# Low parts of weight units: a negated copy and an accumulating DMA in place of a subtraction

## The chip, the cores and the metric

The kernel runs on one core of a Trainium2 chip. What is compared is device time in microseconds of the whole program, one inference step of a two-layer network; the times shown are medians of several runs, and the profile is one execution of its own.

## The reference

One step of a hybrid network over 512 latent and 128 context tokens, 1024 channels wide. Layer 0 mixes tokens by windowed attention beside a convolution module, layer 1 by a gated recurrence in both directions; each layer then has a squared-ReLU MLP of 4096 hidden channels. Every sub-layer is modulated by shift, scale and gate vectors made from a condition vector by large `w_mod` matrices. Cut to what matters:

```
for li in range(2):
    mp, ms = adaln(c_ctx, w_mod[li], b_mod[li]), adaln(c, w_mod[li], b_mod[li])
    h = modulate(y, norm_mix[li], shift, scale)            # RMSNorm, then (1 + scale), + shift
    o = attention_and_conv(h, att_in, att_out, ...)        # li = 0
    o = rg_lru(h, lru_in, lru_out, lru_wa, lru_wx, ...)    # li = 1: conv4, gates, scans both ways
    y = y + gate * o
    y = y + gate2 * (square(relu(modulate(y, ...) @ w_ff1[li])) @ w_ff2[li])
return rmsnorm(y_prompt), rmsnorm(y_sample), new_k, new_v, new_h
```

All of it is in fp32.

## The kernel before

Channels lie on the 128 partitions, the 640 tokens along the free dimension. TensorE multiplies in fp32r, a shortened fp32. To keep fp32 accuracy each operand is cut into a high part (the value rounded to fp32r) and a low part (the value less its high part), and a product is three matmuls: high x high, high x low and low x high. The low part of the weight is named `wlo`, the high part `whi`; those of the activations are `hh` and `hl` (normed input), `fh` and `fl` (hidden), `xh` and `xl` (recurrent gates), `yh` and `yl`.

Weights come in units of 128 x 1024 numbers, 512 KB. `weights` (L101) makes one ready: SyncE loads it into `wraw` (three buffers, and a fourth in the MLPs), ScalarE rounds it into `whi`, and VectorE subtracts: `wlo = wraw - whi`. Both parts have three buffers each (`parts_tile`, L94). A whole unit feeds 48 matmuls (`product`, L115). 118 units are made whole. In the second projection of the MLP (`down`, L814) units are used by halves of 128 x 512, as seven sums and differences of a fast block product; `ready` (L789) cuts each half into the same three buffers, two halves to one. A half feeds 12 matmuls.

The order of work is set by a scheduler that goes by priority and its own cost figures; each engine then runs its list strictly in order. `weights` asks for a priority raised by an `offset`: 4000 in general, 0 for the first six units of attention (L346, L353 and `att_unit`, L381). With 4000 the loading and cutting of a unit stand as early in the lists as their buffers allow.

Places the text speaks of:
- The MLP goes through four groups `g` of eight hidden units `f`. Unit `f = 0` of the next group is multiplied before `down(g)`, and unit `f = 1` inside it, in `between` (L888), just before the last half block, `fourth` (L862). `bu` are two PSUM banks that hold partial sums in `down`.
- The recurrent layer starts with `rec(0)` (L957). Its units are multiplied in the order written in `ORDER`; `gates` (L986) needs ScalarE to free PSUM by `tanh` (tiles `ra`, `ib`), `rec` and `gate_br` need VectorE (tile `bs` is its last step). GpSimd clears the edges of `rp` and copies the last column of each scan into `nst_t` (L1037); it issues no DMA.
- The last four units are those of `ws` (L897), multiplied by halves of the tokens at the very end.

Of the kernel before, what the change touches and what calls it, by code (L numbers as in the profile page):

```python
# [12 lines left out]
AF = mybir.ActivationFunctionType  # L13
ALU = mybir.AluOpType
# [22 lines left out]
def backbone(ctx, tc, vecs, xT, wmod, w_att, w_ao, w_ff1, w_ff2, w_li, w_lo, w_lg, kcT, vc,  # L37
             ident_d, mask_d, rope_d, yo, nkT, nvT, nst):
    nc = tc.nc
# [25 lines left out]
    def sub_lo(out, full, hi):  # L65
        nc.vector.tensor_tensor(out, full, f32(hi), op=ALU.subtract)  # L66
# [18 lines left out]
    def raw_unit(ap):  # L85

        if more and next(unit_) % 4 == 3:
            raw = more[0].tile([128, 1024], F32, name="wraw", tag="wraw")
        else:
            raw = wp.tile([128, 1024], F32, name="wraw", tag="wraw", bufs=3)  # L90
        nc.sync.dma_start(raw, ap)
        return raw

    def parts_tile():  # L94
        return tuple(wp.tile([128, 1024], F32R, name=n, tag=n, bufs=3) for n in ("whi", "wlo"))

    def split(hi, lo, raw):
        nc.scalar.activation(hi, raw, AF.Copy)  # L98
        sub_lo(lo, raw, hi)

    def weights(ap, offset=4000, own=None):  # L101
        with tc.high_priority(offset=offset):
            raw = raw_unit(ap)
            hi, lo = parts_tile() if own is None else (own[:, 0], own[:, 1])
            split(hi, lo, raw)
        return hi, lo


# [235 lines left out]

    first_mods(1, range(W0))
    early = [weights(w_att[0], 0)]  # L346
    first_mods(1, range(W0, 8))
    for k in range(0, 8, 2):
        nc.sync.dma_start(x[:, k:k + 2], xT[:, k:k + 2])
    nm = Norm(ap_, SC[0, 0])  # L350
    for k in range(8):
        nm.scaled(k)
    early += [weights(w_att[1], 0), weights(w_att[2], 0)]  # L353
    for k in range(8):
        nm.square(k)
# [25 lines left out]
    def att_unit(i):  # L381
        wh, wl = weights(w_att[i], 0 if i < WL else 4000)
        p = P2()
        product(p, wh, wl, range(8), rhs)
        return p
# [811 lines left out]
```

## Time and profile before

| | us |
|---|---|
| median of 3 runs | 1446.51 (1446.1 to 1448.87) |
| profiled execution, its own time | 1449.23 |
| span of that execution | 1447.5 |
| TensorE busy | 1409.2 |
| VectorE busy | 1042.9 |
| ScalarE busy | 734.5 |
| GpSimd busy | 89.8 |

The span goes from the first to the last instruction of the program. The profile is read in this order: how busy each engine is, who waited for whom, then the timeline at the places where one unit's parts are made and used. PE is TensorE, DVE VectorE, ACT ScalarE, POOL GpSimd.

### The profile page before, as it was taken

The numbers are of one execution on the slowest core, as the hardware profiler recorded it, in microseconds if no ns is written. First come the engines' busy times: TensorE is split into PE (matmuls) and PEld (weight loads), VectorE is DVE, ScalarE is ACT, GpSimd is POOL, SyncE is SP. The second block draws the span as 40 slices with busy tenths as digits, with TensorE's granted clock in tenths as the row PEclk, the third lists the DMA queues.
The fourth block names the chain that finished last, engine by engine and source line by source line (L and its number), as shares of the span: only waits on it lengthen the run. The fifth ranks groups of instructions, "written<-read, shape, count | busy, mean of one in ns | idle before, by whom it ended". The sixth has DMA issues, their size and how long they took to land.

```text
span 1447.5 us, 23697 instructions
## 1 busy us (share of the span) xinstructions
PE 1409.2 (97%) x9567; PEld 1316.9 (91%) x9567; DVE 1042.9 (72%) x1885; ACT 734.5 (51%) x1174; POOL 89.8 (6%) x126
## 2 busy tenths in 40 slices
PE   6999999999999999999999999999999999999998
PEld 4898674999999999999989999899999999999997
DVE  6699794675765675675588699997676676676673
ACT  5343467455534533533555878835643543543553
POOL 1000760000000000000000023200000000000000
PEclk9998999999999999999999999999999999999999
DMA  8523506224253244334213122122213213113112
GB/s 320 204 74 126 175 1 204 88 95 140 86 183 138 93 142 168 109 131 163 72 59 103 59 73 72 61 74 88 74 46 119 70 59 116 60 59 117 45 59 73
DMA packets 42908, 151.87 MB, mean 105 GB/s; under 512 B 4912, under 2 KB 5680, under 8 KB 42800
## 3 DMA queue, kind: packets, MB, share of 16 engines
q1 hardware_dynamic: 42800, 150.38, 30.1%
q8 instruction: 75, 1.23, 0.3%
q14 instruction: 33, 0.27, 0.1%
HBM read 147.60 MB, written 2.76 MB: 104 GB/s over the span
## 4 chain that ended last, share of the span: by engine, by line
PE 85%; DVE 7%; DMA 3%; ACT 3%; issue 1%; POOL 1%; SPq 0%; ACTq 0%; POOLq 0%; DVEq 0%
PE p L113 65%; PE bu L113 11%; PE p L292 3%; DMA mraw<-in_wmod 3%; PE p L435 2%; DVE wlo L66 1%; PE p L617 1%; DVE xc L976 1%; DVE ib L1035 1%; PE p L613 1%; ACT whi L98 1%; PE p L581 1%; PE p L583 0%; DVE t L1027 0%; DVE ib L1028 0%
## 5 line engine op out<-in xcount | busy, mean ns | idle before, releaser
L98 ACT ACTIVATE whi<-wraw 128x512 fp32r<-128x512 f32 (+1 forms) x327 | 246.5, 779 | 451.8 <-PE p L113 331.5
L113 PE MATMUL p<-hh,whi 128*128 128x320 f32 (+1 forms) x1512 | 462.1, 313 | 2.9 <-ACT hh L186 1.7
L113 PE MATMUL p<-hl,whi 128*128 128x320 f32 (+1 forms) x1512 | 459.8, 311 | 0.2 <-DVE hl L187 0.2
L113 PE MATMUL p<-hh,wlo 128*128 128x320 f32 (+1 forms) x1512 | 349.8, 310 | 0.0
L66 DVE TENSOR_TENSOR wlo<-wraw,whi 128x512 fp32r<-128x512 f32 (+1 forms) x327 | 279.5, 877 | 43.7 <-ACT whi L98 42.2
L113 PEld LDWEIGHTS p<-hh,whi 128*128 128x128 f32 x1512 | 285.6, 189 | 15.4 <-issue 7.8
L113 PEld LDWEIGHTS p<-hl,whi 128*128 128x128 f32 x1512 | 286.0, 189 | 0.9 <-DVE hl L187 0.8
L113 PEld LDWEIGHTS p<-hh,wlo 128*128 128x128 f32 x1512 | 256.4, 189 | 0.9 <-issue 0.8
L113 PE MATMUL p<-fh,whi 128*128 128x320 f32 x528 | 167.0, 316 | 3.9 <-ACT fh L98 1.1
L113 PE MATMUL p<-fl,whi 128*128 128x320 f32 x528 | 163.8, 310 | 2.0 <-DVE fl L66 2.0
L113 PE MATMUL p<-fh,wlo 128*128 128x320 f32 x528 | 163.6, 311 | 0.7 <-DVE wlo L66 0.7
L142 DVE SCALAR_TENSOR_TENSOR x<-p,mod,x 128x320 f32<-128x320 f32 (+2 forms) x228 | 96.1, 448 | 58.6 <-PE p L113 55.8
L268 DVE TENSOR_TENSOR fr<-p,R 128x640 f32<-128x640 f32 x64 | 52.6, 822 | 101.7 <-PE p L113 101.7
L113 PE MATMUL bu<-fh,whi 128*128 128x320 f32 x360 | 113.2, 314 | 0.3 <-ACT bu L841 0.3
L113 PEld LDWEIGHTS p<-fh,whi 128*128 128x128 f32 x528 | 99.9, 189 | 14.0 <-issue 5.1
L113 PE MATMUL bu<-fl,whi 128*128 128x320 f32 x360 | 112.3, 312 | 0.0
L113 PE MATMUL bu<-fh,wlo 128*128 128x320 f32 x360 | 112.1, 311 | 0.0
L740 ACT ACTIVATE fr<-fr,bs 128x512 f32<-128x512 f32 (+1 forms) x128 | 65.2, 555 | 78.5 <-DVE bs L270 78.3
L113 PEld LDWEIGHTS p<-fl,whi 128*128 128x128 f32 x528 | 100.0, 189 | 2.4 <-DVE fl L66 2.4
L113 PEld LDWEIGHTS p<-fh,wlo 128*128 128x128 f32 x528 | 99.6, 189 | 1.5 <-DVE wlo L66 1.5
L416 DVE SCALAR_TENSOR_TENSOR z<-u,vt,z 128x655 f32<-128x655 f32 x90 | 79.3, 904 | 0.4
L292 PE MATMUL p<-mraw,base 128*32 128x256 f32 x768 | 66.0, 418 | 12.8 <-DMA mraw<-in_wmod 7.8
(227 smaller groups left out, 2084.7 us busy)
## 6 DMA issues: line engine op xcount, KB each, us to landing
wraw<-in_w_ff SPq DMA_DIRECT2D x128, 512.0 KB, 3.5
mraw<-in_wmod SPq DMA_DIRECT2D x96, 512.0 KB, 4.1
wraw<-in_w_li SPq DMA_DIRECT2D x16, 512.0 KB, 3.4
wraw<-in_w_att SPq DMA_DIRECT2D x14, 512.0 KB, 3.6
wraw<-in_w_ao SPq DMA_DIRECT2D x8, 512.0 KB, 3.5
wraw<-in_w_lo SPq DMA_DIRECT2D x8, 512.0 KB, 3.4
x<-in_xT SPq DMA_DIRECT2D x4, 640.0 KB, 9.1
wraw<-in_w_lg SPq DMA_DIRECT2D x4, 512.0 KB, 3.5
```

The costliest lines, as they stand in the source:

```text
L66: nc.vector.tensor_tensor(out, full, f32(hi), op=ALU.subtract)
L98: nc.scalar.activation(hi, raw, AF.Copy)
L113: nc.tensor.matmul(o, w, v, start=start, stop=stop, **kw)
L142: nc.vector.scalar_tensor_tensor(v, src[:, a:b], gate[:, n, s:s + 1], v, op0=ALU.mult, op1=ALU.add)
L268: nc.vector.tensor_tensor(hy(o), p[:, :, 0:320], R, op=ALU.mult)
L292: nc.tensor.matmul(p[32 * q:32 * q + 32, half * 256:half * 256 + 256], base[:, kt], raw[:, q * 256:q * 256 + 256], start=(kt == 0), stop=( ...
L416: nc.vector.scalar_tensor_tensor(z, u[:, k:k + 655], wv[:, k:k + 1], z, op0=ALU.mult, op1=ALU.add)
L435: nc.tensor.matmul(p[:, 0:328], dg[:, d], u[:, o + k:o + k + 328], start=(k + i == 0), stop=(k == 30 and i == 2))
L581: nc.tensor.matmul(o, qh[:, g, qs], KH, start=True, stop=False)
L613: nc.tensor.transpose(pt[:, b.kv, g * 128:g * 128 + 128], b.S[g][:, j * 128:j * 128 + 128], ident)
L617: nc.tensor.matmul(pav[c], vv[:, sl, c], th[:, b.kv], start=(j == 0), stop=(j == len(vs) - 1))
L740: nc.scalar.activation(r[:, a:b], r[:, a:b], AF.Relu, bias=bs[:, q:q + 1])
```

## The change

For units asked for with the offset of 4000, `weights` no longer subtracts on VectorE. ScalarE writes the rounded weight into `whi`, then the same rounded weight with the opposite sign into `wlo`; a DMA issued by GpSimd then reads the raw unit from memory a second time and adds it onto `wlo`, which leaves raw less rounded. The six units of the start and all half units keep the subtraction.

```
         with tc.high_priority(offset=offset):
             raw = raw_unit(ap)
             hi, lo = parts_tile() if own is None else (own[:, 0], own[:, 1])
-            split(hi, lo, raw)
+            if offset == 4000:
+                nc.scalar.activation(hi, raw, AF.Copy)
+                nc.scalar.activation(lo, raw, AF.Copy, scale=-1.0)
+                nc.gpsimd.dma_start(lo, ap, accum_op=ALU.add)
+            else:
+                split(hi, lo, raw)
         return hi, lo
```

Lines behind L105 move down by five; the numbers of the buffers change too. ScalarE's list where `down` of the first group of layer 0 ends (the 128x512 rows are the last half blocks, the 128x1024 rows units `f = 1` to 4 of the next group, `fr` and `fh` hidden values), before:

```order
L98 ACTIVATE whi_4225<-wraw_4092 128x512
L98 ACTIVATE whi_4225<-wraw_4094 128x512
L98 ACTIVATE whi_4244<-wraw_4242 128x1024
L98 ACTIVATE whi_4347<-wraw_4345 128x1024
L98 ACTIVATE whi_4416<-wraw_4414 128x1024
L98 ACTIVATE fh_4321<-fr_3718 128x320
L98 ACTIVATE whi_4500<-wraw_4498 128x1024
L740 ACTIVATE fr_4313<-fr_4313,bs_4315 128x512
```

and in the changed kernel:

```order
L98 ACTIVATE whi_4250<-wraw_4117 128x512
L98 ACTIVATE whi_4250<-wraw_4119 128x512
L106 ACTIVATE whi_4269<-wraw_4267 128x1024
L107 ACTIVATE wlo_4270<-wraw_4267 128x1024
L106 ACTIVATE whi_4373<-wraw_4371 128x1024
L107 ACTIVATE wlo_4374<-wraw_4371 128x1024
L106 ACTIVATE whi_4443<-wraw_4441 128x1024
L107 ACTIVATE wlo_4444<-wraw_4441 128x1024
L106 ACTIVATE whi_4528<-wraw_4526 128x1024
L107 ACTIVATE wlo_4529<-wraw_4526 128x1024
L745 ACTIVATE fr_4339<-fr_4339,bs_4341 128x512
```

Each unit has its second activation right behind the first, and the piece of `fh` moves behind the four units.

GpSimd's list in the recurrent layer (`rp` and `nst_t` as above, `ib` the scans' results), before:

```order
L969 MEMSET rp_8841 128x1
L969 MEMSET rp_8841 128x2
L969 MEMSET rp_8841 128x5
L1037 COPY nst_t_7663<-ib_8317 128x1
L1037 COPY nst_t_7663<-ib_8335 128x1
L1037 COPY nst_t_7663<-ib_8412 128x1
L1037 COPY nst_t_7663<-ib_8430 128x1
```

and in the changed kernel:

```order
L108 DMA wlo_8847<-in_w_li 128x1024
L974 MEMSET rp_8904 128x1
L974 MEMSET rp_8904 128x2
L974 MEMSET rp_8904 128x5
L1042 COPY nst_t_7711<-ib_8392 128x1
L108 DMA wlo_8926<-in_w_li 128x1024
L1042 COPY nst_t_7711<-ib_8470 128x1
L1042 COPY nst_t_7711<-ib_8488 128x1
L108 DMA wlo_8986<-in_w_li 128x1024
L108 DMA wlo_9079<-in_w_lg 128x1024
```

The DMAs of the units stand between clears and copies that wait for VectorE.

TensorE's list at the first of the last four units (`p1` its sum, `bu1` the last half block of `down`), before, where these rows are matmuls 22 to 26 of the stretch that the unit begins:

```order
L113 MATMUL p1_13843<-fh_13540,whi_13823 128x320
L113 MATMUL p1_13843<-fl_13541,whi_13823 128x320
L113 MATMUL bu1_9833<-fh_13117,whi_13783 128x320
L113 MATMUL bu1_9833<-fl_13118,whi_13783 128x320
L113 MATMUL bu1_9833<-fh_13117,wlo_13784 128x320
```

and in the changed kernel, from the unit's first matmul on:

```order
L118 MATMUL p1_13955<-fh_13219,whi_13931 128x320
L118 MATMUL p1_13955<-fl_13220,whi_13931 128x320
L118 MATMUL p1_13955<-fh_13219,wlo_13932 128x320
L118 MATMUL p1_13955<-fh_13362,whi_13931 128x320
L118 MATMUL p1_13955<-fl_13363,whi_13931 128x320
L118 MATMUL bu1_9909<-fh_13219,whi_13891 128x320
L118 MATMUL bu1_9909<-fl_13220,whi_13891 128x320
```

The twelve matmuls on `bu` begin after 5 matmuls of the unit; before, they began after 23.

## Rows read from the trace of the kernel before

**Rows 1.** The page, busy microseconds, share of the span and instructions.

```profile
PE 1409.2 (97%) x9567; PEld 1316.9 (91%) x9567; DVE 1042.9 (72%) x1885; ACT 734.5 (51%) x1174; POOL 89.8 (6%) x126
```

**Rows 2.** Waits of TensorE, whole span: total us, times, longest us.

```profile
PE p L113 <- DVE wlo L66: 0.7, 2, 0.6
```

**Rows 3.** Lines by form, whole span: count, busy us, mean ns, idle before.

```profile
L66 DVE TENSOR_TENSOR wlo<-wraw,whi 128x1024 fp32r<-128x1024 f32 x117 | 142.8, 1221 | 16.9 <-ACT whi L98 16.3
L98 ACT ACTIVATE whi<-wraw 128x1024 fp32r<-128x1024 f32 x117 | 123.7, 1058 | 246.3 <-PE p L113 203.0 <-issue 31.2 <-DMA wraw<-in_w_att 8.4
```

**Rows 4.** The chain that ended last, one whole unit: start us, us, what.

```profile
366.61 7.32 PE p L113 x48
```

**Rows 5.** Timeline, a regular unit of layer 1: start us, us, instruction.

```profile
1131.81 1.06 ACT L98 ACTIVATE whi<-wraw 128x1024 fp32r<-128x1024 f32 x1 [2.38 <-PE p L113]
...
1146.70 0.45 PE L113 MATMUL p<-hh,wlo 128*128 128x320 f32 x2
```

**Rows 6.** Timeline, layer 0, second unit of the second hidden group.

```profile
428.64 1.06 ACT L98 ACTIVATE whi<-wraw 128x1024 fp32r<-128x1024 f32 x1 [3.13 <-issue]
...
435.16 0.31 PE L113 MATMUL p<-hh,wlo 128*128 128x320 f32 x1
```

**Rows 7.** Timeline, layer 1, the same place.

```profile
1103.66 1.06 ACT L98 ACTIVATE whi<-wraw 128x1024 fp32r<-128x1024 f32 x1 [2.36 <-issue]
...
1109.43 0.46 PE L113 MATMUL p<-hh,wlo 128*128 128x320 f32 x2
```

**Rows 8.** Timeline, first unit of the recurrent layer.

```profile
774.99 1.06 ACT L98 ACTIVATE whi<-wraw 128x1024 fp32r<-128x1024 f32 x1 [1.36 <-issue]
...
780.76 0.31 PE L113 MATMUL p<-hh,wlo 128*128 128x320 f32 x1
```

**Rows 9.** Timeline, two of the last four units.

```profile
1396.64 1.06 ACT L98 ACTIVATE whi<-wraw 128x1024 fp32r<-128x1024 f32 x1 [1.92 <-issue]
...
1402.11 0.31 PE L113 MATMUL p<-fh,wlo 128*128 128x320 f32 x1
...
1407.15 1.06 ACT L98 ACTIVATE whi<-wraw 128x1024 fp32r<-128x1024 f32 x1 [2.62 <-issue]
...
1411.01 0.31 PE L113 MATMUL p<-fh,wlo 128*128 128x320 f32 x1
```

**Rows 10.** DMA view: the queue's load; issues with size and us to landing.

```profile
q1 hardware_dynamic: 42800, 150.38, 30.1%
...
wraw<-in_w_ff SPq DMA_DIRECT2D x128, 512.0 KB, 3.5
mraw<-in_wmod SPq DMA_DIRECT2D x96, 512.0 KB, 4.1
```

**Rows 11.** Lines by form: GpSimd's column copies.

```profile
L1037 POOL COPY nst_t<-ib 128x1 f32<-128x1 f32 x16 | 31.9, 1994 | 69.3 <-DVE ib L1035 69.1
```

**Rows 12.** Timeline, recurrent layer: a GpSimd copy, VectorE, a unit's low part.

```profile
893.28 7.07 POOL L1037 COPY nst_t<-ib 128x1 f32<-128x1 f32 x1 [2.33 <-DVE ib L1035]
...
900.23 0.81 DVE L268 TENSOR_TENSOR rt<-p,R 128x640 f32<-128x640 f32 x1
...
905.90 0.45 PE L113 MATMUL p<-hh,wlo 128*128 128x320 f32 x2
```

**Rows 13.** Timeline, recurrent layer, TensorE behind its two longest gaps.

```profile
809.15 0.39 PE L113 MATMUL p<-xh,whi 128*128 128x322 f32 x1 [1.80 <-DVE bs L270]
...
921.29 0.41 PE L113 MATMUL p<-xh,whi 128*128 128x322 f32 x1 [1.80 <-ACT ra L998]
```

**Rows 14.** Windows behind those gaps: busy us by engine, granted clock, DMA share.

```profile
809.80:813.20 3.40, 3.40 (x15) 3.40 (x14) 1.70 (x3) 3.19 (x6) 0.00 (x0) 0.50 0.12 49
...
922.40:925.90 3.50, 3.50 (x16) 3.49 (x15) 3.50 (x5) 3.21 (x5) 1.97 (x2) 0.51 0.00 0
```

**Rows 15.** Window over the recurrent layer: PE, PEld, DVE, ACT, POOL busy.

```profile
797.00:941.00 144.00, 137.37 (x884) 133.68 (x883) 122.06 (x174) 121.55 (x148) 30.77 (x30) 0.98 0.19 67
```

**Rows 16.** Lines by form in that window: whole units' high parts.

```profile
L98 ACT ACTIVATE whi<-wraw 128x1024 fp32r<-128x1024 f32 x19 | 19.9, 1050 | 3.9 <-PE p L113 3.9
```

## The prediction

> **What bounds the kernel now.** I read the page's busy times first. TensorE is busy for 1409.2 of the 1447.5 us of the span, VectorE for 1042.9 and ScalarE for 734.5 [rows 1]. So an edit that takes no matmul away can win only from TensorE's 38 idle microseconds and from what its clock loses behind them. The second view is the list of waits: on the low parts that the change makes differently, TensorE's matmuls waited 0.7 us in the whole run, in two places [rows 2]. The low parts are off the path now. The question is by how much they are early, and the timeline says that.
>
> **What is removed and added.** 112 of the 118 whole units change (118 less the six of the start that are built with another offset). Each loses a VectorE subtraction of 1.22 us and gets a second ScalarE activation of the form of its first, 1.06 us [rows 3], and a DMA of 512 KB on GpSimd's queue. VectorE loses 112 x 1.22 = 137 us, ScalarE gains 112 x 1.06 = 119 us and stands at 853 of 1447 us. By itself neither moves the end: VectorE's subtraction had no one waiting, and ScalarE has 700 us free. What counts is when the low part is there. Before, that was one subtraction, 1.22 us, after the high part; now it is 1.06 us (the negated copy) plus L, the time from the end of that copy to the landing of the DMA.
>
> **How long L may be.** A unit of 48 matmuls takes TensorE 7.3 us [rows 4], and three buffers give two units of lead. In layer 1 the high part starts at 1131.81, the first matmul on the low part at 1146.70 [rows 5]. The room for L is 1146.70 - 1131.81 - 2 x 1.06 = 12.8 us. Most units look so. Nine places do not:
> - After each second projection of layer 0 (three times) the next unit gets its buffer late, because half units of 12 matmuls pass through the same three buffers: 435.16 - 428.64 - 2.12 = 4.4 us [rows 6].
> - The same in layer 1, three times: 1109.43 - 1103.66 - 2.12 = 3.65 us [rows 7].
> - The first unit of the recurrent layer: 780.76 - 774.99 - 2.12 = 3.65 us [rows 8].
> - Two of the four last units: 1402.11 - 1396.64 - 2.12 = 3.35 us, and 1411.01 - 1407.15 - 2.12 = 1.74 us [rows 9]. At the second one the order helps: twelve matmuls on `bu`, whose buffer this unit waits for, stand after 5 matmuls of the unit before and not after 23. At 0.15 us each [rows 4] that is 18 x 0.15 = 2.7 us earlier, so 4.4 us.
>
> The order lists show no filler for TensorE at the first seven; it is strictly in order, and behind the matmul that waits stand all the rest.
>
> **What L is.** No row shows an accumulating DMA, or any DMA of GpSimd. The nearest row is the plain load of the same bytes by SyncE, 3.5 us from issue to landing [rows 10]; that is the lower end. The queue moved 150.38 MB in 30.1% of 1447.5 us, 0.345 MB per us, so of the 3.5 us the 0.524 MB take 1.5 and 2.0 are fixed. An accumulating transfer reads the old value as well as the weight. I count the moving twice: 2.0 + 3.0 = 5.0 us. GpSimd's share is unknown: its column copies take 2.0 us in the mean [rows 11], and one took 7.07, held until VectorE came to an instruction that reads PSUM at 900.23 [rows 12]. I take 1.0 for it, half the mean, since a descriptor list is not read from a tile: L = 6.0 us. The upper end is 5.0 + 7.1 = 12.1. That other loads run beside it (`mraw` takes 4.1 us and not 3.5, same rows 10) may add 0.6.
>
> The Trainium skill, page "DMA: Bandwidth & Descriptors", section "Anatomy of one DMA — SWDGE (gpsimd) path", gives for a DMA of GpSimd 2.0 us plus the bytes over 436 KB per us. By that a plain one of 512 KB would take 3.2 us, an estimate from the page; no run here shows it, SyncE's 3.5 is near it, and by it L would be below every room but 1.74 and the sum zero. That is the second rival below.
>
> **The sum.** At L = 6.0: 3 x (6.0 - 4.4) = 4.8; 3 x (6.0 - 3.65) = 7.05; 2.35; 2.65; 1.6. Together 18.5 us in nine waits of 1.6 to 2.65 us. The units after such a wait are not late too: their buffers and their use move together.
>
> Each wait has a second price. In the recurrent layer TensorE stood idle twice for 1.80 us [rows 13], and behind each it was granted 0.50 and 0.51 of the clock, 1.2 instead of 2.4 GHz, for 3.4 us [rows 14]; that loses 1.7 us. All nine waits are about as long or longer: 9 x 1.7 = 15.3 us.
>
> In the recurrent layer the DMAs are queued on GpSimd behind copies that wait for scans. One copy ends at 893.28 + 7.07 = 900.35, the unit's DMA stands behind it, and its low part is used at 905.90 [rows 12]: 5.55 us of room, so 0.45 us of wait. Its other queue neighbours have more room.
>
> The same stage has ScalarE at 121.55 of 144 us and VectorE at 122.06 [rows 15]. Nineteen units are built there [rows 16]: ScalarE goes to 121.55 + 19 x 1.06 = 141.7 of 144, VectorE to about 99. Of the two gaps of 1.80 us one is ended by VectorE and one by ScalarE [rows 13]; I let the one go and the other grow by as much, zero. The bounds are -7.0 us (both gaps and their clock go: 2 x 3.5) and +20 us (every new activation on the path).
>
> Sum: 18.5 + 15.3 + 0.45 = 34 us. The profiled execution took 1449.23 us (span 1447.5 and 1.7 around it), so 1483; the median of the runs, 1446.51, is 2.7 lower, so I forecast **1481 us**.
>
> **Rivals.**
> 1. *GpSimd is held up.* The copy of 7.07 us [rows 12] speaks for it: 128 single elements, held while VectorE worked. Against it: VectorE is idle for 28% of the span [rows 1], and each idle moment would let GpSimd in. At L = 12 the nine waits cost 9 x 12 - 35.6 = 72.4 us (35.6 is the sum of the nine rooms), the clock 15.3: 1534 us. It decides from L = 8 on. Past 12.8 every third unit would wait as well. The Trainium skill, page "SBUF — State Buffer", section "SBUF: two separate sides", has the mechanism: while VectorE runs an instruction that takes both shared ports, GpSimd can't write descriptors and its DMA waits. The copy agrees in kind; that a DMA of GpSimd does so is shown by no run here.
> 2. *The landing is hidden.* L is 3.5 to 4, as for SyncE's load; at most 9 x 0.3 us are left, and the time stays at 1446.5. For it: the fixed 2.0 us dominate. Against it: the old value must be read, and GpSimd must hand on.
> 3. *Not slower but faster: VectorE's relief in the recurrent layer.* With L below 4, the gap behind VectorE's `bs` goes, and the one behind ScalarE if the freed scans let its inputs come sooner: 1446.5 - 7.0 = 1439.5. It decides only if no wait of the nine is over half a microsecond. Against it: ScalarE at 141.7 of 144.
> 4. *ScalarE becomes the bound of the recurrent layer.* With the landing hidden, half of the 20 us come onto the path: 1456.5. For it: its activations free the PSUM that TensorE waits for. Against it: 141.7 of 144 still fits.
>
> **Chances.** Forecast (L from 5 to 8) 0.56; rival 1 0.14; rival 2 0.12; rival 3 0.08; rival 4 0.10. The forecast's own range: at L = 5 the waits are 9 x 5 - 35.6 = 9.4 us, half of them long enough to cost clock, 7.7: 1464; at L = 8 36.4 + 15.3 + 2.5 = 54: 1500. The range of 1446 to 1520 leaves out rival 3 and the upper part of rival 1. What is within 0.2% (2.9 us) can't be told from no change: same is rival 2, 0.12; faster is rival 3, 0.08; slower is the rest, 0.80.
>
> **What would show it.** In the new profile the waits list would have TensorE waiting for the DMA of `wlo` about nine times for 1.5 to 3 us: at the start of the second unit of a hidden group in both layers, at the start of the recurrent layer and at the last four units; the granted clock would be at half behind them. GpSimd's DMA of `wlo` would show some 6 us to landing. The row of 128x1024 subtractions on VectorE would be down from 117 to 6. I am wrong if the landing takes under 4 us, if the recurrent layer changes its length by more than 5 us, or if TensorE waits in regular units too.

## The result, and the profile after

The changed kernel took 1502.7, 1503.9 and 1510.7 us, against 1446.3 us in the median for the kernel before: a ratio of 1.0408, with a 95% interval of 1.0368 to 1.0448, some 59 us more. (A fourth execution of it was disturbed and is left out of the ratio.) The direction was forecast, 1481 us was not: the loss was 34 us by the sum and is 59. The profiled execution is the one of 1502.7, with a span of 1500.9 us, 53.4 more than the profiled one before; that is less than 59 because the one was the shortest of its three and the other 2.9 us above its median. The page's busy times, to be set beside [rows 1]:

```profile
PE 1421.2 (95%) x9567; PEld 1328.2 (88%) x9567; DVE 916.2 (61%) x1773; ACT 832.1 (55%) x1287; POOL 177.7 (12%) x238
```

VectorE lost 127 us, ScalarE gained 98, and neither is the point. TensorE is idle for 1500.9 - 1421.2 = 79.7 us, before 38.3: 41.4 more. It is also busy for 12.0 us more with the same matmuls, which is the clock: its busy time inside the stretches of half clock grew by 26.2 us, outside them it fell by 14.2. 41.4 + 12.0 is the whole 53.4. The list of waits (total us, times, longest) names the idle part; [rows 2] had 0.7 us on `wlo`:

```profile
PE p L118 <- DMA wlo<-in_w_ff: 31.4, 11, 4.0
PE p L297 <- DMA mraw<-in_wmod: 10.6, 14, 2.8
PE p L118 <- ACT ra L1003: 9.2, 4, 5.4
PE p L118 <- DMA wlo<-in_w_li: 2.6, 1, 2.6
PE p L118 <- DVE bs L275: 2.0, 5, 0.8
```

Before, `mraw` was 7.8, `ra` 3.8 and `bs` 2.9. So: 34.0 us for the landing of `wlo`, 5.4 for `ra`, 2.8 for `mraw`, 0.9 back from `bs`; together 41.3. The timeline at the places of [rows 6], [rows 7], [rows 8] and [rows 9] (start, us, instruction, idle before it):

```profile
428.14 1.06 ACT L106 ACTIVATE whi<-wraw 128x1024 fp32r<-128x1024 f32 x1 [3.13 <-issue]
429.10 1.04 ACT L107 ACTIVATE wlo<-wraw 128x1024 fp32r<-128x1024 f32 x1
430.17 0.33 SPq L91 DMA_DIRECT2D wraw<-in_w_ff  x1
430.44 0.86 POOL L108 DMA_DIRECT2D wlo<-in_w_ff  x1 [69.90 <-ACT wlo L107]
430.59 0.38 SPq L318 DMA_DIRECT2D mraw<-in_wmod  x1
438.68 0.56 PE L118 MATMUL p<-hh,wlo 128*128 128x320 f32 x2 [3.85 <-DMA wlo<-in_w_ff]
...
800.67 0.41 PE L118 MATMUL p<-hh,wlo 128*128 128x320 f32 x1 [2.60 <-DMA wlo<-in_w_li]
...
1129.01 1.06 ACT L106 ACTIVATE whi<-wraw 128x1024 fp32r<-128x1024 f32 x1 [2.35 <-issue]
1129.97 1.04 ACT L107 ACTIVATE wlo<-wraw 128x1024 fp32r<-128x1024 f32 x1
1131.04 3.80 SPq L91 DMA_DIRECT2D wraw<-in_w_ff  x2
1131.31 0.86 POOL L108 DMA_DIRECT2D wlo<-in_w_ff  x1 [63.60 <-ACT wlo L107]
1138.03 0.41 PE L118 MATMUL p<-hh,wlo 128*128 128x320 f32 x1 [3.10 <-DMA wlo<-in_w_ff]
...
1157.98 0.41 PE L118 MATMUL p<-hh,wlo 128*128 128x320 f32 x1 [2.20 <-DMA wlo<-in_w_ff]
...
1451.06 0.41 PE L118 MATMUL p<-fh,wlo 128*128 128x320 f32 x1 [2.11 <-DMA wlo<-in_w_ff]
...
1459.61 0.42 PE L118 MATMUL p<-fh,wlo 128*128 128x320 f32 x1 [2.40 <-DMA wlo<-in_w_ff]
```

The negated copy ends at 430.14; GpSimd issues the DMA 0.3 us later and spends 0.86 us on it; it lands at 438.63. L is 8.5 us there, and in layer 1 1137.98 - 1131.01 = 7.0. One row between them matters later: SyncE starts the next raw load at 430.17, 0.27 us ahead of the accumulating DMA. The negated copy is the last reader of the raw buffer, so its end releases both at once. The DMA part of the page, beside [rows 10]:

```profile
q1 hardware_dynamic: 42800, 150.38, 31.3%
q0 software_dynamic: 16128, 58.73, 21.6%
...
wraw<-in_w_ff SPq DMA_DIRECT2D x128, 512.0 KB, 4.1
mraw<-in_wmod SPq DMA_DIRECT2D x96, 512.0 KB, 4.2
wlo<-in_w_ff POOLq DMA_DIRECT2D x67, 512.0 KB, 7.9
```

A landing takes 7.9 us from issue in the median, from 5.4 to 11.0. And the clock behind such a wait, as in [rows 14]:

```profile
1139.60:1142.90 3.30, 3.30 (x15) 3.30 (x14) 0.00 (x0) 0.00 (x0) 0.00 (x0) 0.50 0.51 101
```

The granted clock is at half (1.2 GHz) for 3.4 us; over the run it is so for 66.5 us in 15 stretches, before for 35.5 us in 6. Nine of the 15 stand behind waits on `wlo`.

### The profile page after: what moved, and what is told of

It is laid out like the page before. It is cut to its first block, busy times and chain, and to the rows that moved or that the text cites. A ratio compares the mean times of both kernels' runs of the same rounds, so it can differ in the third digit from the quotient of the medians.

```text
span 1500.9 us, 23987 instructions
## 1 busy us (share of the span) xinstructions
PE 1421.2 (95%) x9567; PEld 1328.2 (88%) x9567; DVE 916.2 (61%) x1773; ACT 832.1 (55%) x1287; POOL 177.7 (12%) x238
## 3 DMA queue, kind: packets, MB, share of 16 engines
q0 software_dynamic: 16128, 58.73, 21.6%
## 4 chain that ended last, share of the span: by engine, by line
PE 72%; DMA 9%; issue 9%; DVE 6%; ACT 4%; POOL 0%; SPq 0%; POOLq 0%; DVEq 0%; ACTq 0%
PE p L118 57%; PE bu L118 6%; DMA wlo<-in_w_ff 6%; PE p L297 3%; DMA mraw<-in_wmod 3%; PE p L440 2%; DVE wlo L66 1%; PE p L622 1%; PE p L618 1%; ACT whi L98 1%; DVE t L1032 1%; DVE ib L1033 0%; DVE ib L1040 0%; ACT t L1027 0%; ACT wlo L107 0%
## 5 line engine op out<-in xcount | busy, mean ns | idle before, releaser
L118 PE MATMUL p<-hh,whi 128*128 128x320 f32 (+1 forms) x1512 | 467.6, 316 | 3.1 <-ACT hh L191 1.7
L118 PE MATMUL p<-hh,wlo 128*128 128x320 f32 (+1 forms) x1512 | 355.6, 314 | 29.5 <-DMA wlo<-in_w_ff 26.9
L118 PEld LDWEIGHTS p<-hh,whi 128*128 128x128 f32 x1512 | 290.1, 192 | 15.7 <-issue 6.6
L118 PEld LDWEIGHTS p<-hl,whi 128*128 128x128 f32 x1512 | 290.4, 192 | 0.7 <-DVE hl L192 0.5
L106 ACT ACTIVATE whi<-wraw 128x1024 fp32r<-128x1024 f32 x111 | 117.4, 1058 | 257.9 <-PE p L118 145.9
L98 ACT ACTIVATE whi<-wraw 128x512 fp32r<-128x512 f32 (+1 forms) x216 | 128.9, 636 | 225.3 <-PE p L118 144.4
L66 DVE TENSOR_TENSOR wlo<-wraw,whi 128x512 fp32r<-128x512 f32 (+1 forms) x216 | 144.0, 701 | 34.1 <-ACT whi L98 33.1
L108 POOL DMA_DIRECT2D wlo<-in_w_ff x67 | 57.8, 863 | 823.0 <-ACT wlo L107 818.9
L107 ACT ACTIVATE wlo<-wraw 128x1024 fp32r<-128x1024 f32 x111 | 115.7, 1042 | 0.0
L118 PEld LDWEIGHTS p<-fh,whi 128*128 128x128 f32 x528 | 99.9, 189 | 14.1 <-issue 6.3
```

The source lines that it names most:

```text
L107: nc.scalar.activation(lo, raw, AF.Copy, scale=-1.0)
L108: nc.gpsimd.dma_start(lo, ap, accum_op=ALU.add)
L118: nc.tensor.matmul(o, w, v, start=start, stop=stop, **kw)
```

## The experiments

Theory A at the start: the loss is the landing at the units with little room, and the clock behind these waits. Theory B: 58.7 MB more traffic slows everything. Twelve kernels were run.

**1. Only the close units go back.** `weights` gets a flag `acc`; without it a unit subtracts.

```
-            if offset == 4000:
+            if offset == 4000 and acc:
...
+            wh, wl = weights(w_ff1[l, g * 8 + f], acc=g == 0 or f not in (1, 3))
+        wh, wl = weights(w_li[(j // 4) * 8 + j % 4], acc=j != 0)
+            ws = [weights(w_ff2[1, 28 + i], own=own if i == 3 else None, acc=False) for i in range(4)]
```

> Twelve or thirteen units go back to the subtraction: units 1 and 3 of the hidden groups that follow a down projection in both layers, the first unit of the recurrent layer and the last four. All others keep the accumulating DMA. Theory A (the loss is the landing of the accumulating DMA at the units with little room): the twelve waits on the low part (34.0 us) and the nine half-clock stretches behind them (9 x 1.7 = 15.3 us) go, and what is left is the recurrent layer's own part, 5.4 us more idle behind ScalarE and 1.7 of clock: 1451 to 1456 us. Theory B (the 58.7 MB of additional transfers slow the other loads everywhere): under half of the loss goes, 1475 us or more.

It was 17 units (12 + 1 + 4; the expectation miscounts). Measured: 1452.8 us, ratio 1.0047 (1.0035 to 1.006). Some nine tenths of the loss hang on 17 of 112 units; the 95 others still move 49.8 MB and cost 5 to 9 us. Theory B falls.

**2. The reverse: only these 17 accumulate** (the flag the other way round).

> The reverse of the first experiment: only the 17 units with little room (units 1 and 3 after a down projection, 12 of them, the first of the recurrent layer, the last four) are built by the accumulating DMA, 95 subtract. Theory A/F: first units wait as in the changed kernel (11.9 us in layer 0, 9.9 in layer 1, 2.6 to 4.1 at the recurrent layer, 4.5 at the end, each of most with 1.7 us of clock); the third units no longer wait, since no second accumulating DMA lies on top of theirs; the recurrent layer keeps its length: 1484 to 1494 us. Theory B (total traffic): 1446.8 plus 17/112 of 60 us, about 1456.

Measured: 1501.0 us, ratio 1.0369 (1.0353 to 1.0384): above the range expected, and nearly the whole loss with 15% of the DMAs. The waits:

```profile
PE p L118 <- DMA wlo<-in_w_ff: 35.1, 12, 5.6
PE p L118 <- DMA wlo<-in_w_li: 3.2, 1, 3.2
```

One part of the expectation failed: four of the six third units still wait, 0.7 to 1.3 us each, so a second accumulating DMA on top is only part of what makes theirs late. And in layer 1 the landing is longer here (7.8 to 8.2 us) than with all units changed (6.7 to 7.1). Why is not settled.

**3. The DMA left out, ScalarE's second activation kept.**

```
-                nc.gpsimd.dma_start(lo, ap, accum_op=ALU.add)
```

> The DMA is left out: the low part stays the negated high part, and the raw weight is not added. ScalarE's second activation stays in all 112 units. Theory A: the twelve waits go; if the recurrent layer's gaps come from ScalarE's added 1.04 us per unit they stay, 1451 to 1455 us. Rival C (they come from GpSimd's queue or from the landing): 1446 us or less. Theory B (traffic) also gives 1446.

Measured: 1449.7 us, ratio 1.0016 (1.0006 to 1.0025). The median is a little under the expected range, but the recurrent layer's gaps are all there, as in the changed kernel to a tenth:

```profile
PE p L117 <- ACT ra L1002: 9.2, 4, 5.4
```

So they don't come from the DMAs; what is left is ScalarE's second activation and the order that came with it. What ScalarE does there shows in the changed kernel's timeline:

```profile
931.71 1.28 ACT L1053 ACT_TABLE_LOAD   x1
933.00 1.02 ACT L1053 ACTIVATE gt<-gt,bs 128x512 f32<-128x512 f32 x2
934.02 1.28 ACT L1027 ACT_TABLE_LOAD   x1
935.32 2.36 ACT L1027 ACTIVATE t<-t 128x2576 f32<-128x2576 f32 x1
...
940.21 1.28 ACT L1053 ACT_TABLE_LOAD   x1
941.51 1.01 ACT L1053 ACTIVATE gt<-gt,bs 128x512 f32<-128x512 f32 x2
942.43 0.78 ACT L1003 ACTIVATE ra<-p,hb 128x644 f32<-128x644 f32 x1
...
943.26 0.64 PE L118 MATMUL p<-xh,whi 128*128 128x322 f32 x1 [5.40 <-ACT ra L1003]
```

and at the same place before (TensorE waits 1.14 us for the `ra` of the last row; the second gap of [rows 13] comes 5.8 us later, behind another `ra`):

```profile
907.20 1.28 ACT L1022 ACT_TABLE_LOAD   x1
908.49 2.36 ACT L1022 ACTIVATE t<-t 128x2576 f32<-128x2576 f32 x1
910.75 0.72 ACT L978 ACTIVATE xh<-xc 128x644 fp32r<-128x644 f32 x1
911.50 1.28 ACT L1048 ACT_TABLE_LOAD   x1
...
914.66 0.78 ACT L998 ACTIVATE ra<-p,hb 128x644 f32<-128x644 f32 x1
```

With longer work in its list the scheduler put a piece of the gelu (`gt`) ahead of the square roots (`t`), so ScalarE changes its function table three times and not twice, 1.28 us each, ahead of the `ra` for which TensorE waits. Two second activations (L107, 1.04 us each) stand in the same stretch. In the 19.2 us ahead of the matmul behind the longest gap, ScalarE (the fourth figure behind the comma) was busy for 16.5 us before and has no room left in the changed kernel:

```profile
902.00:921.20 19.20, 16.34 (x108) 15.65 (x106) 16.55 (x26) 16.53 (x21) 2.10 (x2) 1.00 0.24 83
...
924.00:943.20 19.20, 13.86 (x94) 13.60 (x92) 11.33 (x17) 19.12 (x24) 1.86 (x3) 0.96 0.61 138
```

**4. Only the recurrent layer accumulates** (`acc=False` everywhere else).

> Only the units of the recurrent layer (w_li, w_lg, w_lo) are built by negated copy and accumulating DMA; the MLPs, the attention and the last four units subtract. Theory A: the wait at the first unit of the layer (2.6 us and 1.7 of clock) and the longer gaps behind ScalarE (5.4 and 1.7) stay, 1446.5 + 11.4 = 1458 us. Rival C (these gaps are an echo of the waits before them, not ScalarE's load): only the first unit's wait, 1450 to 1451 us. Rival D (VectorE's relief helps the layer): below 1446.

Measured: 1456.9 us, ratio 1.0071 (1.0058 to 1.0083), 1 us from theory A's figure. The first unit waits 4.1 us, the gaps behind `ra` are again 9.2.

**5. Accumulating only where the room is wide**, in the MLPs and the attention.

> The accumulating DMA only where the room is 9 us or more: regular units of both MLPs and the attention; the close units, the recurrent layer and the last four subtract. Theory A: nothing waits, 1446.5 us within 2. Theory B (traffic): 1452 us or more, with longer waits on mraw. A gain (below 1443) would say that VectorE's relief is worth something in the MLPs.

Measured: 1448.9 us, ratio 1.0015 (1.0006 to 1.0024). No wait on a DMA of `wlo` is left, and `ra` is back at 3.8. 68 DMAs that nobody waits for cost 0.9 to 3.5 us (theory A allowed 2), and VectorE's relief brings nothing. The waits on `mraw` are 13.1 us, but 14.1 in experiment 3, which has none of these DMAs, so they don't speak for theory B.

**6. As 1, but in the recurrent layer VectorE writes the negated copy**, and the DMAs stay.

```
+                if dve:
+                    nc.vector.tensor_scalar(lo, raw, -1.0, None, op0=ALU.mult)
+                else:
                     nc.scalar.activation(lo, raw, AF.Copy, scale=-1.0)
```

> Like the first experiment (17 close units subtract), and in the recurrent layer VectorE, not ScalarE, writes the negated copy; the accumulating DMAs stay there. If the 4.5 us by which the recurrent layer grew come from ScalarE's order (one activation table load more and the gelu in front of the square roots), they go: 1446 to 1449 us. If they come from the DMAs or GpSimd's queue there: 1451 to 1454 us, as in the first experiment.

Measured: 1447.6 us, ratio 1.0005 (0.9996 to 1.0013). The gelu (L1056) is behind the square roots (L1030) again, with two table loads ahead of the `ra` at 912.63:

```profile
905.17 1.28 ACT L1030 ACT_TABLE_LOAD   x1
906.46 2.36 ACT L1030 ACTIVATE t<-t 128x2576 f32<-128x2576 f32 x1
...
909.47 1.28 ACT L1056 ACT_TABLE_LOAD   x1
```

So ScalarE was the cause, and the DMAs and GpSimd's queue cost nothing that shows there. The run takes ScalarE's second activations and the changed order away together; it doesn't part the two.

**7. A plain DMA of GpSimd, without the addition** (so the low part is the whole raw weight).

```
-                nc.gpsimd.dma_start(lo, ap, accum_op=ALU.add)
+                nc.gpsimd.dma_start(lo, ap.bitcast(F32R))
```

> GpSimd's DMA copies the raw weight onto the low part without adding (the subtraction is left out); same bytes, same queue, same place in the program. Theory A1 (the accumulating transfer is long because each byte goes twice, and the more so beside other loads): landing 4 to 5 us from issue and not 8, so L about 4.7, waits only at the nine closest places and under 1 us, 1452 to 1462 us. Rival A2 (a DMA of GpSimd is this long whatever it does): landing 7 to 8, the waits and the time of the changed kernel, about 1505 us.

Measured: 1466.1 us, ratio 1.0124 (1.0096 to 1.0153), a little above A1's range, far from A2. Layer 1, the same place:

```profile
1121.26 3.80 SPq L91 DMA_DIRECT2D wraw<-in_w_ff  x2
1121.52 0.53 POOL L108 DMA_DIRECT2D wlo<-in_w_ff  x1 [63.94 <-ACT wlo L107]
...
1126.08 0.42 PE L118 MATMUL p<-hh,wlo 128*128 128x320 f32 x1 [0.92 <-DMA wlo<-in_w_ff]
```

It lands 4.5 us after issue beside the same raw load, where the accumulating one takes 6.7. At the end of the program, where nearly nothing runs beside it, 3.8 against 5.4. In layer 0, with the `mraw` loads beside it, even the plain one takes 6.1 to 7.6.

**8. The raw weight read from SBUF and not from memory.**

```
-                nc.gpsimd.dma_start(lo, ap, accum_op=ALU.add)
+                nc.gpsimd.dma_start(lo, raw, accum_op=ALU.add)
```

> The accumulating DMA reads the raw weight from the tile in SBUF that SyncE has loaded, and not again from memory. Theory A1 (read of the old value and write are what is long): landing within 1 us of 8, time within 1% of the changed kernel's 1505, perhaps longer since the raw buffer is held until the landing and the next raw load starts later. Rival (the second read of memory is what is long): landing 5 us, time below 1480.

Measured: 1475.1 us, ratio 1.0195 (1.0176 to 1.0213), median landing 5.0 us. Theory A1 as put there falls: it expected 8. But the run changes two things, as the timeline shows:

```profile
1125.88 0.86 POOL L108 DMA_DIRECT2D wlo<-wraw  x1 [63.60 <-ACT wlo L107]
...
1130.40 0.42 PE L118 MATMUL p<-hh,wlo 128*128 128x320 f32 x1 [0.90 <-DMA wlo<-wraw]
```

The landing takes 4.5 us, but no raw load starts beside it, since its buffer is held until the landing. The next run parts the two.

**9. Memory again as the source, the raw buffer held by a small piece.**

```
-                nc.gpsimd.dma_start(lo, ap, accum_op=ALU.add)
+                nc.gpsimd.dma_start(lo[:, 0:896], ap[:, 0:896], accum_op=ALU.add)
+                nc.gpsimd.dma_start(lo[:, 896:1024], raw[:, 896:1024], accum_op=ALU.add)
```

> The accumulating DMA takes columns 0 to 895 from memory as before, and a second one takes the last 128 columns from the raw tile in SBUF, so that the raw buffer is held until the landing and the load that follows into it can't start together with the accumulating DMA. Theory F (an accumulating transfer alone takes 5.4 us; it takes 6.7 to 8.2 at the close places because the raw buffer that the negated copy frees starts the next raw load 0.3 us before it): in layer 1 the landing falls to 5.5 us or less, as with the raw weight read wholly from SBUF, and the waits there to about 2 us or under; total 1478 to 1490 us. Rival G (the source decides: memory is slow to read for this DMA, SBUF is fast): landing in layer 1 stays at 6.5 us or more, total 1500 or more.

Measured: 1483.4 us, ratio 1.0251 (1.0237 to 1.0265).

```profile
1128.79 0.87 POOL L108 DMA_DIRECT2D wlo<-in_w_ff  x1 [62.71 <-ACT wlo L107]
1129.33 1.22 POOL L109 DMA_DIRECT2D wlo<-wraw  x1
...
1134.18 0.53 PE L119 MATMUL p<-hh,wlo 128*128 128x320 f32 x2 [1.76 <-DMA wlo<-in_w_ff]
```

No raw load starts at 1128.8, and the transfer from memory, of seven eighths of the bytes, lands in 5.0 to 5.3 us in layer 1. That is theory F. The same run shows it a second way, at equal bytes in one kernel. A raw load was issued within 0.9 us of 36 of its DMAs from memory, with no `mraw` load beside them: they took 6.3 to 7.9 us to land. Of the 45 with neither, 36 took 4.9 to 5.6. What is left to the source is 0.5 to 0.8 us (4.5 from SBUF).

**10. Two DMAs of 512 columns for each unit.**

```
+                for c in (slice(0, 512), slice(512, 1024)):
+                    nc.gpsimd.dma_start(lo[:, c], ap[:, c], accum_op=ALU.add)
```

> Each accumulating DMA is split into two of 512 columns. GpSimd spends about 0.86 us more per unit. If the time to landing is mostly the moving (theory A1, 4 to 6 of 8 us), the first half lands 2 to 3 us earlier, and TensorE, which starts with the first columns, waits 1 to 2 us less at each place: 1475 to 1490 us. If it is mostly a fixed time, both halves land after about 8 us and the time is 1505 or more.

Measured: 1485.4 us, ratio 1.0268 (1.0243 to 1.0293). The first half lands after 6.1 to 7.1 us at the close places of the MLPs, the second a good microsecond behind; TensorE waits 2.6 to 2.9 us there. Half the bytes save 0.5 to 1.5 us of the landing. Both halves and the raw load are under way together there; that this is the reason was not tested.

**11. The negated copy written first.**

```
-                nc.scalar.activation(hi, raw, AF.Copy)
                 nc.scalar.activation(lo, raw, AF.Copy, scale=-1.0)
                 nc.gpsimd.dma_start(lo, ap, accum_op=ALU.add)
+                nc.scalar.activation(hi, raw, AF.Copy)
```

> ScalarE writes the negated copy first and issues the high part behind it, so the DMA starts 1.06 us earlier against the buffer. Theory A (each wait is L less the room): every wait shrinks by 1.0 us, 12 x 1.0 = 12 us, and some fall under the length that costs clock: 1485 to 1495 us. Rival: the high part is now late by 1.06 us where TensorE reaches it early, and the sum stays, 1500 to 1507.

Measured: 1508.6 us, ratio 1.0423 (1.0393 to 1.0452). It tested nothing at the close places: the scheduler put the high part first all the same.

```profile
431.14 1.06 ACT L108 ACTIVATE whi<-wraw 128x1024 fp32r<-128x1024 f32 x1 [3.13 <-issue]
432.10 1.04 ACT L106 ACTIVATE wlo<-wraw 128x1024 fp32r<-128x1024 f32 x1
```

**12. As 6, with everything outside the recurrent layer subtracting.**

> The accumulating DMA only in the recurrent layer, without its first unit, with the negated copy written by VectorE; everything else subtracts. In the run before, this stage (first hidden units of layer 1 to the last pair of its MLP) was 604.0 us long and not 607.0. If that is a gain of the order of the work and not of one execution, the time is 1443 to 1445 us. If it is scatter, or given back elsewhere: 1446.5 within 1.5.

Measured: 1446.5 us, ratio 0.9994 (0.9986 to 1.0003). The stretch is 604.0 us in this profile too, but no gain is left in the times that can be told from none. The 607.0 hold the two stretches of half clock of [rows 14], the 604.0 none. The profiled execution of the kernel before had a mean granted clock of 0.988, most of its others beside these runs 0.991 or 0.992, so the 3 us may belong to that execution. No version beat the kernel before.

## Why the prediction was right in direction and short in size

*Which places wait: eight of nine right, and some missed.* Eight of the nine waits on the list came: three in layer 0, three in layer 1, one at the recurrent layer, one at the first of the last four units. Of these four, the list's second place was the unit that is multiplied third, and it did not wait. The one multiplied second did, for 2.40 us. Its rows before (high part, first matmul on the low part) give it 1407.48 - 1401.42 - 2.12 = 3.94 us of room by the prediction's own subtraction, and the list left it out:

```profile
1401.42 1.04 ACT L98 ACTIVATE whi<-wraw 128x1024 fp32r<-128x1024 f32 x1
...
1407.48 0.31 PE L113 MATMUL p<-fh,wlo 128*128 128x320 f32 x1
```

Each of the eight is L less the room, to a quarter of a microsecond:

| place | room, forecast | L, measured | wait, measured |
|---|---|---|---|
| layer 0, three | 4.40 | 8.49, 8.68, 8.62 | 3.85, 4.04, 3.97 |
| layer 1, three | 3.65 | 6.97, 7.17, 7.43 | 3.10, 3.29, 3.55 |
| recurrent layer | 3.65 | 6.47 | 2.60 |
| end, first | 3.35 | 5.69 | 2.11 |

*The term that failed: L = 6.0 us.* For a transfer with little beside it the sum was good: fixed 2.0, moving twice 3.0, GpSimd 1.0 made 6.0, and 5.7 was measured at the end of the program. "That other loads run beside it may add 0.6" was the mistake: at layer 1's close places, beside the raw load that the negated copy itself sets off, it was 1.3 to 1.7 us (6.7 to 7.1 against 5.4), and in layer 0, with the loads of `mraw`, 2.8 to 3.0. The trace's packet records show where it begins. At the two places where no load starts with the DMA (956.45 and 1445.62) its first packet moves 1.6 us after issue; in the 31 cases where one raw load does, and no other accumulating DMA is under way, 2.3 to 2.8 us. The rest scatters: the 16 DMAs with that raw load alone beside them landed after 6.2 to 8.3 us, in the median 6.6, and why is open. The row that tells of the raw load was in reach: the order of events at a freed buffer. These eight waits and the one of 2.40 came to 28.9 us in place of 18.5.

*What was left out.* The third unit after a down projection had 7.4 to 9 us of room and was counted among the regular ones. Its DMA and the next unit's are issued 1.9 us apart (1148.43 and 1150.33), land after 9.5 and 10.1 us; at three of the six such places TensorE waited, 5.1 us together.

*The clock.* Forecast 15.3 us for nine waits, measured 12.0 of longer matmuls in all. The rule taken from two rows, that each wait is followed by 3.4 us at half clock, holds for nine of the twelve waits: behind the 2.20 us at 1157.98, the 2.11 at 1451.06 and one of 1.06 no such stretch follows.

*The recurrent layer.* Forecast zero with bounds of -7 and +20; measured 5.4 us more behind `ra` and 0.9 less behind `bs`. From TensorE's gap ahead of the layer to the one at the end of layer 1's MLP it is 607.0 us in the kernel before and 611.5 in experiment 3. That is the second term that failed: zero for ScalarE, where 4.5 us came. Experiment 6 settles that ScalarE was the reason. Over the whole stage its load still fits, as the prediction said (135.8 of 148.0 us from 818 to 966); in the stretch ahead of the longest gap it does not (19.1 of 19.2 us), with two second activations (2.1 us) and, by the new order, one function table load more and a piece of the gelu (2.3 us). How much each of the two costs is not parted. ScalarE's order list of this layer would have shown the new order beforehand. GpSimd's queue, 0.45 us in the sum, cost nothing that shows.

*The sum, term by term, in the profiled execution:* 28.9 + 5.1 + 12.0 + 4.5 + 2.8 (`mraw`) = 53.3 of 53.4 us. `mraw` is not the change's alone: in experiment 4, where nothing differs before the recurrent layer, it waited 13.0 us.

*The rivals.* GpSimd is not held up: 109 of 112 DMAs are issued 0.29 to 0.32 us behind the negated copy and take 0.85 to 0.89 us of it, the first 1.03; the three others stand behind its copies in the recurrent layer. VectorE made no difference to the first packet: of the 31 cases above, it moves after 2.3 to 2.7 us in the seven where VectorE is busy all that time, after 2.4 and 2.5 in the two where it is idle. The mechanism that the Trainium skill, "SBUF — State Buffer", section "SBUF: two separate sides", gives for rival 1 shows in none of them; whether VectorE ran instructions there that take both ports no run shows. The hidden landing (rival 2) fell by the runs: even the plain DMA of experiment 7 waited. Rival 3 fell: no version gained. Rival 4 was right in part: with the DMA left out the recurrent layer is 4.5 us longer behind ScalarE, not 10. The formula of the Trainium skill, "DMA: Bandwidth & Descriptors", section "Anatomy of one DMA — SWDGE (gpsimd) path", gives 3.2 us for a plain DMA of 512 KB, an estimate from the page; this case has 3.8 nearly alone and 4.5 beside one load, and the measurement decides. To count the moving twice for an accumulating one fits: for the same 58.73 MB the queue's packets took 21.6% of the span, plain 11.4%. The Trainium skill, "Collectives: The Full Stack", section "The bandwidth ceiling: the fold count and why AG ≠ RS ≠ AR", tells of one collective, ReduceScatter, that its addition reads two sources and that it comes to half of AllGather's rate. These shares, a ratio of 1.9, agree.

## What to carry to other kernels

When an engine's work is handed to a DMA, take the room at every place from the timeline and compare it with the landing under the load that will lie beside it, above all the one that the same event sets off: here the end of the last reader of a buffer started the next load into it. The few units behind a change of buffer size decide the time; the 95 others cost 5 to 9 us, most of it in the recurrent layer behind ScalarE, and gave nothing, since the relieved engine was not the bound. Where a change adds work to an engine, look at the stretch just ahead of each wait and not at the share over the stage, and read the new order for function table loads.

## What the runs showed of the hardware that was not expected

- An accumulating DMA of 512 KB from memory lands 5.4 us after issue nearly alone. With one raw load alone beside it, it takes 6.2 to 8.3 (at layer 1's close places, where the next unit's transfers follow after 3.2 us, 6.7 to 7.1), in layer 0 beside a raw load and one of `mraw` 8.2 to 8.4, and up to 11.0 where two such DMAs are issued 1.9 us apart. A plain one takes 3.8 nearly alone, 4.5 to 4.6 at layer 1's close places and 6.1 to 7.6 at those of layer 0. From SBUF nearly alone the accumulating one takes 4.5.
- A load issued 0.3 us ahead of such a DMA puts off its first packet, from 1.6 us after issue to between 2.3 and 2.8.
- Issuing it costs GpSimd 0.86 us, a plain one 0.53, nearly the same for every DMA of a kind but the first.
- Two halves take hardly less time to land than the whole: 6.1 to 7.1 us for the first half where the whole took 6.7 to 8.4.
- Waits of TensorE of 2.7 to 2.8 us were followed by half clock once of three times in layer 0 of experiment 8, those of 3.1 us and more on `wlo` in the changed kernel every time; of its waits on `wlo` of 1.8 to 2.2 us one was and two were not. One of 3.27 us in experiment 7 and one of 3.02 in experiment 9 were not.
